# Sample convolution as POOL products with DVE sums, and prompt softmax normalised at its output, in a hybrid decoder step

## The chip, the core and the metric

The kernel runs on one core of a Trainium2 chip. The core has a matrix engine (TensorE, PE in the rows), two elementwise engines (VectorE, DVE; GpSimd, POOL), a table engine (ScalarE, ACT), a queue processor that starts transfers (SyncE, SP), and 16 DMA engines. Every engine runs its own instructions in the order in which they were written and waits on semaphores where it needs another's result. Only POOL can start the gathering transfers with a table of row indices; each costs POOL time of its own. The metric is the device time of one execution in microseconds. The granted clock of TensorE is told as a share of full speed: it changes between 1.2 and 2.4 GHz.

## What is computed

One layer of a decoder, for one prompt of 1024 tokens and for 8 sequences with 8 new tokens each (the sample): half a feed-forward, then attention beside a convolution, an output projection, and another half feed-forward.

```python
u = rms_norm(x) @ w_in              # query latent 384 | kv latent 256 | rope key 32 | conv 2 x 512
# group A: latent attention, 8 heads. Prompt: causal over 1024 tokens.
# Sample: over 4096 cached tokens in 32 pages of each sequence, and the 8 new ones
s = (q_abs @ c_kv.T + q_pe @ k_pe.T) * SM_SCALE
o = softmax(mask(s)) @ c_kv ; attn_out = o @ w_uv
# group B: convolution of width 31 along the tokens, 512 channels
g = ga * sigmoid(gb)
ext = concat([conv_state, g])       # 30 earlier rows (zeros for the prompt)
y = depthwise_conv(ext, w_dw) + b_dw    # y[t, ch] = b[ch] + sum over k of w_dw[k, ch] * ext[t + k, ch]
conv_out = silu(layer_norm(y))
x = x + concat([rms_norm(attn_out), rms_norm(conv_out)]) @ w_out
```

All data is fp32. The outputs are the new hidden states and the new cache entries.

## The kernel before

In time the kernel is: first feed-forward (to some 760 us in the trace), in-projection (to 905), the **sample stage** (905 to 1278), the **prompt attention** (1278 to 1487), out-projection (to 1640) and the second feed-forward. Large matrix products are done with fewer multiplications by adding operands first, so that three matmuls (lines 127, 128 and 129, `mm3`) stand for a product; DVE, ACT and POOL make the operand sums.

The order on every engine is settled when the program is built. A planner (`fl`) keeps a clock of estimated nanoseconds: generators yield the cost of the piece just written, `fl.add` starts a piece that runs beside the others, `fl.spend` lets the planned time pass, `fl.wait` lets it pass until pieces are done. A changed cost so moves the pieces of other work in the queues, and nothing is reordered on the chip.

**Sample stage.** `mgen` (line 1520) walks 32 steps, each with 1024 cached tokens of one sequence, two tiles of keys a half. `qk` multiplies queries with the keys `kst`, three quarters of which SP loads and one quarter POOL gathers (lines 1036, 1032), and DVE moves the scores to an SBUF tile `Ssb` from the pool `sb` (tag "S", LAG+2 = 7 buffers). `expo` and `trans` follow 4 and 5 steps later, and `pv` (line 1478) multiplies with the latents `cst` 6 steps later. All 128 `cst` tiles are gathered by POOL (line 1416, 7 buffers): when PE has read two tiles, the next two loads may start. Into this stream the planner fills other PE work: `w2` (line 1242, the conv inputs, matmuls `u<-h,w`, for four groups of 128 channels) and then `pprep` (keys and values of the prompt).

`conv_chunk` (line 1147) puts the convolution of one channel group into the queue `conv`: for each of 31 taps one DVE operation over the prompt's 1024 positions (input `gx`) and one over the sample's 64 (input `ge`, 8 sequences of 38 rows). The first tap is a `tensor_scalar` with the bias, the others are `scalar_tensor_tensor`, output `zc`. `conv_run` (line 1160) emits them one by one at their planned costs of 1150 and 200 ns, and goes on with the layer norm of the convolution (`lnorm`, line 1176) in three column groups of 364, 364 and 360 tokens; its end is a tanh on ACT and two POOL `tensor_tensor` (tiles `th` and `zc`, lines 1225 to 1230) for each of the four channel groups.

**Prompt attention.** 16 units, each a block of 256 queries (i = 0 to 3) and a pair of heads p. `stage_a` makes the queries `qf` (PE, then DVE with a table out of PSUM), `stage_b` the scores of the four (head e, half v) parts into SBUF tiles `P`, with L = 128 to 1024 keys. `soft` (line 1616) is the minimum, ACT's exp with the row sum (line 1620), DVE's reciprocal (line 1622), and a scaling of all of P by it: on DVE for v = 0 (line 1627), on ACT for v = 1 (line 1625, `P<-P,s` of line 116). `stage_c` (line 1630) transposes P in 128 x 128 pieces on PE (`T_`, line 1643) into a PSUM bank of kind "t" (three banks), moves them to SBUF (`pt`, DVE at line 1650 or ACT), and multiplies with the values (`PV`, line 1658) into the single bank of kind "o"; ACT moves that to `at` (line 1670). The units overlap: while unit u makes its scores, unit u+1 makes its queries and unit u-1 is in `stage_c`. The functions follow as they were.

Of the kernel before, what the change touches and what calls it, by code (L numbers as in the profile page):

```python
# [103 lines left out]
def body(ctx, tc, A):  # L104
# [1014 lines left out]
    def qhead():  # L1119
# [14 lines left out]
        for c in range(3):  # L1134
            m = 96 if c < 2 else 64
            for e in range(2):
# [5 lines left out]
                yield 850.0  # L1142


    conv = deque()

    def conv_chunk(i, gx, ge):
        for k in range(CW):
            wk = wdw[:, i, k:k + 1]
            for o, g, ns in ((zc[:, i, 0:S], gx[:, k:k + S], 1150.0),  # L1150
                             (zc[:, i, S:N].rearrange("p (b t) -> p b t", t=T), ge[:, :, k:k + T], 200.0)):
                if k == 0:
                    conv.append((ns, lambda o=o, g=g, wk=wk: dve.tensor_scalar(
                        out=o, in0=g, scalar1=wk, scalar2=b_dw[:, i:i + 1], op0=ALU.mult, op1=ALU.add)))
                else:
                    conv.append((ns, lambda o=o, g=g, wk=wk: stt(o, g, wk, o, ALU.mult, ALU.add)))

    share = [0.0]

    def conv_run():  # L1160
        done = 0
        while done < 4 * 2 * CW:
            if conv:
                ns, op = conv.popleft()
                op()
                done += 1
                yield ns / share[0]
            else:
                yield 300.0
        yield from lnorms()  # L1170
# [71 lines left out]
    def w2():  # L1242
        for i in range(4):
            while len(conv) > 2 * (CW if i > 1 else 2 * CW):
                yield None
# [30 lines left out]
    es_kv, es_q = ExitStack(), ExitStack()  # L1276
    kT, at_ = [], {}

# [126 lines left out]
    cp, sb, ptp, sm = op("cp", CBUF), op("sb", LAG + 2), op("ptp", 2), op("sm", 2)  # L1405
    B = {}

    def load_c():
# [133 lines left out]
    for d in mgen():  # L1542
        fl.spend(d)
        due += d * (KV_RATE if at_ else FILL_RATE)
        while fill is not None and due > 0.0:
# [38 lines left out]
    def stage_a(u):  # L1584
        i, p = units[u]
        U[u] = dict(q=[], P={}, pt={}, soft=[])
        for e in range(2):
# [10 lines left out]
    def stage_b(u):  # L1598
        i, p = units[u]
        for e in range(2):  # L1600
            for v in range(2):
                qt = 2 * i + v
                L = (qt + 1) * 128
                P = pp.tile([128, S], F32, tag="P", name="P")
                mn, s_, rs = (sm.tile([128, 2], F32, tag=f"s{j}", name=f"s{j}") for j in range(3))
                for j, k0 in enumerate(range(0, L, 512)):
# [5 lines left out]
                U[u]["P"][e, v] = P  # L1612
                U[u]["soft"].append(fl.add(soft(P, L, v, mn, s_, rs), L * 1.69 + 900.0))
                yield L * 1.69

    def soft(P, L, v, mn, s_, rs):
        if L > 512:
            tt(mn[:, 0:1], mn[:, 0:1], mn[:, 1:2], ALU.min)
            yield 300.0
        act.activation(out=P[:, :L], in_=P[:, :L], func=AF.Exp, scale=-1.0, bias=mn[:, 0:1], accum_out=s_[:, 0:1])  # L1620
        yield 900.0 +  0.4 * L
        dve.reciprocal(out=rs[:, 0:1], in_=s_[:, 0:1])
        if v:
            yield 300.0
            acopy(P[:, :L], P[:, :L], rs[:, 0:1])
        else:
            dve.tensor_scalar(out=P[:, :L], in0=P[:, :L], scalar1=rs[:, 0:1], scalar2=None, op0=ALU.mult)
        yield 0.0

    def stage_c(u):  # L1630
        i, p = units[u]
        fl.wait(*U[u]["soft"])
        o = bank("o")[:, :256]
        P, pt = U[u]["P"], U[u]["pt"]

        def T_(e, jj):
# [26 lines left out]
        for jj in range(i + 3):  # L1663
            if jj <= i:
                T_(1, jj)
                yield 430.0
            if jj > 1:
                PV(jj - 2)
                yield 860.0
        acopy(at[:, p, i * 256:i * 256 + 256], o)  # L1670
        U.pop(u)
# [10 lines left out]
    for u in range(len(units) + 1):  # L1682
# [8 lines left out]
        if u:  # L1691
            other.append(stage_c(u - 1))
            cost += (units[u - 1][0] + 1) * 1720.0
        done = 0.0
# [101 lines left out]
KBUF, CBUF = 6, 7  # L1796
LAG = 5
BIG = 3e38

# [95 lines left out]
```

## Time and profile before

| | us |
|---|---|
| three runs, median (lowest, highest) | 2372.63 (2364.92, 2373.29) |
| the profiled execution, its own time | 2358.99 |
| its span from first to last instruction | 2357.2 |
| PE busy in the span | 2178.0 (92%) |
| DVE, ACT, POOL busy | 1568.2, 843.8, 1063.3 |
| mean granted clock of TensorE | 0.967 |

The profiled execution is 13.6 us below the median of the runs, and 1.8 us of it lie outside its span. A busy engine says little by itself: what a stage is worth is read from the waits of PE in that stage and from what ended them, and PE's clock falls where it had to wait. All rows named below are from this one execution.

### The profile page before, as it was taken

Reading aid. Unit: us, or ns where it says so; the run is one execution under the profiler, and the core shown is the slowest. Engines: PE = TensorE matmul, PEld = TensorE weight load, DVE = VectorE, ACT = ScalarE, POOL = GpSimd, SP = SyncE. Lnnn points to the kernel's source line nnn. Section 1 sums busy time; section 2 is a strip of 40 time slices with the busy share of each in tenths; the row PEclk is TensorE's granted clock in tenths of the full one; section 3 lists DMA queues with packets and bytes.
Section 4 is the critical chain, followed back from the end, with each engine's and each line's share of the span. In section 5 each row is a group of like instructions: output and inputs, shape, how many; then the busy total and the mean of one; then the engine's idle time right before and its main releaser. Section 6 shows DMA issues by size and latency. Waiting matters only on the chain. (4 is left out here: it accounts for less than half of the span.)

```text
span 2357.2 us, 42356 instructions
## 1 busy us (share of the span) xinstructions
PE 2178.0 (92%) x15714; PEld 1999.7 (85%) x15714; DVE 1568.2 (67%) x3061; ACT 843.8 (36%) x1759; POOL 1063.3 (45%) x995
## 2 busy tenths in 40 slices
PE   6989999999999898997688999899799999999997
PEld 6989999999999796785455765799799999999996
DVE  7976666666565666996533776577866656766567
ACT  4332222234344421211233656543332222334343
POOL 3446676631134303675455322343456777411234
PEclk8999999999999998998888999999999999999998
DMA  4126676648654434888575000452166666458653
GB/s 147 51 82 212 203 228 200 210 144 291 225 193 161 128 124 133 227 244 234 169 225 157 14 1 18 139 194 92 61 195 209 212 219 211 131 194 285 210 170 122
DMA packets 252527, 392.69 MB, mean 167 GB/s; under 512 B 26912, under 2 KB 188064, under 8 KB 252192
## 3 DMA queue, kind: packets, MB, share of 16 engines
q1 hardware_dynamic: 153184, 261.23, 35.2%
q10 hardware_dynamic: 85824, 85.75, 10.6%
q0 software_dynamic: 13312, 43.00, 6.3%
q8 instruction: 124, 2.03, 0.4%
q14 instruction: 83, 0.68, 0.1%
HBM read 299.71 MB, written 90.19 MB: 165 GB/s over the span
## 5 line engine op out<-in xcount | busy, mean ns | idle before, releaser
L110 DVE TENSOR_TENSOR wh<-wst,wh 128x512 fp32r<-128x512 f32 x355 | 302.7, 861 | 281.6 <-ACT wh L116 280.7
L110 POOL TENSOR_TENSOR ts<-ts 128x272 f32<-128x272 f32 (+1 forms) x352 | 309.3, 879 | 314.4 <-DMA ts<-a_dram 197.7
L127 PE MATMUL gu<-h,wh 128*128 128x272 f32 x1248 | 361.9, 290 | 11.9 <-DVE m L110 9.8
L128 PE MATMUL gu<-h,wh 128*128 128x272 f32 x1248 | 361.0, 289 | 4.0 <-DVE h L110 4.0
L129 PE MATMUL gu<-h,wh 128*128 128x272 f32 x1248 | 360.9, 289 | 1.2 <-DVE wh L110 1.2
L116 ACT ACTIVATE wh<-wst 128x512 fp32r<-128x512 f32 x355 | 217.9, 624 | 398.7 <-PE d L129 167.2
L127 PE MATMUL d<-h,wh 128*128 128x272 f32 x1232 | 355.5, 289 | 0.0
L128 PE MATMUL d<-h,wh 128*128 128x272 f32 x1232 | 353.9, 287 | 0.0
L129 PE MATMUL d<-h,wh 128*128 128x272 f32 x1232 | 353.8, 287 | 0.0
L127 PE MATMUL gu<-t,wh 128*128 128x272 f32 x936 | 273.5, 292 | 18.3 <-DVE sg L110 11.5
L129 PE MATMUL gu<-t,wh 128*128 128x272 f32 x936 | 271.7, 290 | 3.0 <-DVE wh L110 3.0
L128 PE MATMUL gu<-t,wh 128*128 128x272 f32 x936 | 271.2, 290 | 2.7 <-DVE t L110 2.7
L127 PEld LDWEIGHTS gu<-h,wh 128*128 128x128 f32 x1248 | 235.8, 189 | 14.7 <-DVE m L110 12.4
L128 PEld LDWEIGHTS gu<-h,wh 128*128 128x128 f32 x1248 | 235.9, 189 | 4.7 <-DVE h L110 4.7
L129 PEld LDWEIGHTS gu<-h,wh 128*128 128x128 f32 x1248 | 235.7, 189 | 1.4 <-DVE wh L110 1.4
L127 PEld LDWEIGHTS d<-h,wh 128*128 128x128 f32 x1232 | 231.6, 188 | 0.4
L128 PEld LDWEIGHTS d<-h,wh 128*128 128x128 f32 x1232 | 231.6, 188 | 0.2
L129 PEld LDWEIGHTS d<-h,wh 128*128 128x128 f32 x1232 | 231.4, 188 | 0.0
L1416 POOL DMA_INDIRECT cst<-in_cN,c_rep x128 | 142.5, 1113 | 182.2 <-DVE qx L1141 83.5
L127 PEld LDWEIGHTS gu<-t,wh 128*128 128x128 f32 x936 | 177.7, 190 | 22.4 <-DVE sg L110 14.4
L127 PE MATMUL u<-h,w 128*128 128x364 f32 (+3 forms) x528 | 183.0, 347 | 2.0 <-ACT h L116 2.0
L129 PEld LDWEIGHTS gu<-t,wh 128*128 128x128 f32 x936 | 177.7, 190 | 3.2 <-DVE wh L110 3.2
(260 smaller groups left out, 4884.9 us busy)
## 6 DMA issues: line engine op xcount, KB each, us to landing
wst<-in_wgu SPq DMA_DIRECT2D x88, 512.0 KB
kst<-in_kT SPq DMA_DIRECT2D x192, 144.0 KB
t_dram<-ts ACTq DMA_DIRECT2D x44, 544.0 KB
ts<-in_wd SPq DMA_DIRECT2D x88, 256.0 KB
a_dram<-acc ACTq DMA_DIRECT2D x78, 272.0 KB
wst<-s_dram SPq DMA_DIRECT2D x40, 512.0 KB
ast<-t_dram SPq DMA_DIRECT2D x66, 272.0 KB
s_dram<-ts ACTq DMA_DIRECT2D x44, 384.0 KB
```

The lines of the kernel that those rows point to most:

```text
L110: eng.tensor_tensor(out=out, in0=a, in1=b, op=op)
L116: act.activation(out=out, in_=a, func=AF.Copy, scale=scale)
L127: pe.matmul(out, ah, bh, start=first, stop=False)
L128: pe.matmul(out, ah, bl, start=False, stop=False)
L129: pe.matmul(out, al, bh, start=False, stop=last)
L1416: pool.indirect_dma_start(out=t.rearrange("p a c -> p (a c)"), out_offset=None, in_=A["cN"], in_offset=bass.IndirectOffsetOnAxis(ap=cidx[: ...
```

## The change

Two things are changed. **In the sample's convolution** the 31 DVE operations of a channel group on 64 positions become four POOL multiplications, four DVE reductions and one DVE addition of the bias. Each multiplication takes two sequences: an overlapping view of `ge` (for each of 8 positions the 31 inputs that its taps read) times the 31 taps, broadcast, gives 2 x 8 x 31 = 496 products a partition; the tile `cwin` for them comes from the score pool `sb`, tag "S". They are put into the queue `conv` behind the prompt's taps 8, 13, 18 and 23, and each is summed one such place later. The queue of a channel group has 40 entries in place of 62. The prompt's taps stay as they are. `at_` is moved up, and the test for the values becomes `"V" in at_`, with the same meaning.

**In the prompt attention** P stays unscaled. The four row sums of a unit stand in one tile; DVE takes the reciprocal of the four at once and spreads each over 64 columns (`rw`), PE transposes the two 128 x 128 halves into a bank of kind "t", ACT moves that to SBUF (`rb`), and the move of the output to `at` becomes a DVE multiplication `at = o * rb`. The planned costs follow: `soft` ends with the exp, and `stage_c` has 220 ns more.

```diff
 def conv_chunk(i, gx, ge):
     for k in range(CW):
         wk = wdw[:, i, k:k + 1]
-        for o, g, ns in ((zc[:, i, 0:S], gx[:, k:k + S], 1150.0),
-                         (zc[:, i, S:N].rearrange("p (b t) -> p b t", t=T), ge[:, :, k:k + T], 200.0)):
...
+        o, g = zc[:, i, 0:S], gx[:, k:k + S]
...
+        if k in SPOTS:
+            sconv(i, SPOTS.index(k), ge)
+def sconv(i, j, ge):
+    if 0 < j <= DB // 2:
+        o = zc[:, i, S + 2 * (j - 1) * T:S + 2 * j * T].rearrange("p (b t) -> p b t", t=T)
+        conv.append((600.0, lambda: dve.tensor_reduce(out=o, in_=prod.pop((i, j - 1)), axis=AX.X, op=ALU.add)))
+    if j < DB // 2:
+        def make():
+            g = ge[:, 2 * j:2 * j + 2, 0:T]
+            win = bass.AP(g.tensor, g.offset, [*g.ap, [1, CW]])
+            w = wdw[:, i].unsqueeze(1).unsqueeze(1).to_broadcast([128, 2, T, CW])
+            t = at_["sb"].tile([128, 512], F32, tag="S", name="cwin")[:, :2 * T * CW]
+            t = prod[i, j] = t.rearrange("p (b t k) -> p b t k", b=2, k=CW)
+            tt(t, win, w, ALU.mult, pool)
+        conv.append((0.0, make))
+    if j == DB // 2 + 1:
+        o2 = zc[:, i, S:N]
+        conv.append((200.0, lambda: dve.tensor_scalar(out=o2, in0=o2, scalar1=b_dw[:, i:i + 1], scalar2=None, op0=ALU.add)))
...
-    while done < 4 * 2 * CW:
+    while done < 4 * (CW + DB + 1):
...
+SPOTS = (8, 13, 18, 23, 28, 30)
...
 def soft(P, L, mn, s_):
...
-    dve.reciprocal(out=rs[:, 0:1], in_=s_[:, 0:1])
-    if v:
-        yield 300.0
-        acopy(P[:, :L], P[:, :L], rs[:, 0:1])
-    else:
-        dve.tensor_scalar(out=P[:, :L], in0=P[:, :L], scalar1=rs[:, 0:1], scalar2=None, op0=ALU.mult)
...
 def stage_c(u):
+    dve.reciprocal(out=rs.rearrange("p v e -> p (v e)"), in_=U[u]["sums"].rearrange("p v e -> p (v e)"))
+    wide = sm.tile([128, 2, 2, 64], F32, tag="rw", name="rw", bufs=2)
+    dve.tensor_copy(wide, rs.unsqueeze(3).to_broadcast([128, 2, 2, 64]))
+    rb = sm.tile([128, 256], F32, tag="rb", name="rb", bufs=2)
+    def spread_sums():
+        ps = bank("t")[:, :256]
+        for v in range(2):
+            pe.transpose(ps[:, v * 128:v * 128 + 128], wide[:, v].rearrange("p e d -> p (e d)"), ident)
+        acopy(rb, ps)
...
+            if jj == 1:
+                spread_sums()
+                yield 220.0
...
-        acopy(at[:, p, i * 256:i * 256 + 256], o)
+        tt(at[:, p, i * 256:i * 256 + 256], o, rb, ALU.mult)
```

The instructions stand as follows on the engines. First POOL early in the sample stage, before (the rows give line, operation, tiles and size; `mn` and `sums` are the sample attention's statistics):

```order
L1425 MEMSET mn 128x5
L1426 MEMSET sums 128x5
L1032 DMA kst<-in_kT,c_prep 96x384 x8
L1425 MEMSET mn 128x5
L1426 MEMSET sums 128x5
L1032 DMA kst<-in_kT,c_prep 96x384 x6
L1416 DMA cst<-in_cN,c_rep 128x512 x4
```

The same place with the change:

```order
L1449 MEMSET mn 128x5
L1450 MEMSET sums 128x5
L1032 DMA kst<-in_kT,c_prep 96x384 x2
L110 TENSOR_TENSOR cwin<-ge,c_wdw 128x496
L1032 DMA kst<-in_kT,c_prep 96x384 x2
L110 TENSOR_TENSOR cwin<-ge,c_wdw 128x496
L1032 DMA kst<-in_kT,c_prep 96x384 x4
L110 TENSOR_TENSOR cwin<-ge,c_wdw 128x496
L1449 MEMSET mn 128x5
L1450 MEMSET sums 128x5
```

The products stand between the gathers, four to each channel group, 16 in all.

POOL at the end of the sample stage, before (`th` and `zc` are the end of the layer norm of the first 364 tokens):

```order
L1032 DMA kst<-in_kT,c_prep 96x384 x2
L1416 DMA cst<-in_cN,c_rep 128x512 x25
L110 TENSOR_TENSOR th<-th,zc 128x364
L110 TENSOR_TENSOR zc<-zc,th 128x364
L110 TENSOR_TENSOR th<-th,zc 128x364
L110 TENSOR_TENSOR zc<-zc,th 128x364
```

The same place with the change:

```order
L1032 DMA kst<-in_kT,c_prep 96x384 x2
L1440 DMA cst<-in_cN,c_rep 128x512 x20
L110 TENSOR_TENSOR th<-th,zc 128x364
L110 TENSOR_TENSOR zc<-zc,th 128x364
L110 TENSOR_TENSOR th<-th,zc 128x364
L110 TENSOR_TENSOR zc<-zc,th 128x364
L1440 DMA cst<-in_cN,c_rep 128x512 x4
L110 TENSOR_TENSOR th<-th,zc 128x364
L110 TENSOR_TENSOR zc<-zc,th 128x364
L1440 DMA cst<-in_cN,c_rep 128x512
L110 TENSOR_TENSOR th<-th,zc 128x364
L110 TENSOR_TENSOR zc<-zc,th 128x364
```

The convolution is planned to end earlier, so its layer norm comes earlier in the queue: four of the multiplications now stand ahead of the last five gathers, and two more ahead of the last one.

DVE around the last unit of the prompt attention, before (`s` are the sums, `pt` the transposed P):

```order
L1622 RECIPROCAL s_17303<-s_17302 128x1
L1627 TENSOR_SCALAR P<-P,s_17303 128x896
L110 TENSOR_TENSOR s_17326<-s_17326 128x1
L1622 RECIPROCAL s_17328<-s_17327 128x1
L1650 COPY pt_17356<-t 128x512
L1650 COPY pt_17370<-t 128x512
```

The same place with the change:

```order
L110 TENSOR_TENSOR s_17155<-s_17155 128x1
L110 TENSOR_TENSOR at<-o,rb 128x256
L1654 RECIPROCAL rs<-s_16902 128x4
L1656 COPY rw<-rs 128x256
L1679 COPY pt_17184<-t 128x512
L1679 COPY pt_17198<-t 128x512
L110 TENSOR_TENSOR at<-o,rb 128x256
```

The scaling of P is gone, one reciprocal of the four sums and its spreading stand ahead of the copies out of the "t" banks, and the move of the output is now in DVE's queue.

## Rows read from the trace of the kernel before

**Rows 1.** Busy time of the engines by stretch of time, from the view of windows: stretch, length, PE, PEld, DVE, ACT, POOL, then the granted clock, the share of the DMA engines and GB/s.

```profile
905.00:960.00 55.00, 45.73 (x292) 34.91 (x291) 42.83 (x76) 7.06 (x13) 25.30 (x25) 0.88 0.62 172
960.00:1098.00 138.00, 135.86 (x991) 105.21 (x990) 124.91 (x237) 27.80 (x68) 99.27 (x95) 0.99 0.88 245
1098.00:1200.00 102.00, 60.28 (x354) 39.24 (x352) 46.86 (x87) 22.92 (x55) 41.61 (x39) 0.77 0.59 176
1200.00:1278.00 78.00, 68.11 (x445) 41.22 (x441) 25.19 (x76) 30.51 (x75) 50.25 (x54) 0.93 0.78 233
1278.00:1487.00 209.00, 195.39 (x1196) 133.86 (x1196) 146.62 (x512) 131.13 (x312) 57.61 (x59) 0.97 0.04 14
```

**Rows 2.** Waits of PE in the sample stage, from the view of waits of three stretches, in order: 960 to 1098, 1098 to 1200, 1200 to 1278. Columns: us in total, times, longest.

```profile
PE s L1434 <- DMA kst<-in_kT,c_prep: 1.3, 1, 1.3
...
PE s L1434 <- DMA kst<-in_kT: 36.1, 4, 12.6
PE s L1434 <- DMA kst<-in_kT,c_prep: 5.6, 1, 5.6
...
PE o L1491 <- DMA cst<-in_cN,c_rep: 6.2, 9, 1.9
```

**Rows 3.** The convolution on DVE, 905 to 1278, groups by operation and shape: count, busy us in all, mean ns of one, idle time before.

```profile
L113 DVE SCALAR_TENSOR_TENSOR zc<-gx,c_wdw,zc 128x1024 f32<-128x1024 f32 x120 | 153.0, 1275 | 0.0
L113 DVE SCALAR_TENSOR_TENSOR zc<-ge,c_wdw,zc 128x64 f32<-128x64 f32 x120 | 33.1, 276 | 0.0
```

**Rows 4.** Waits of POOL, 960 to 1098 (first row) and 1098 to 1200 (the other two).

```profile
POOL cst L1416 <- PE o L1491: 17.6, 13, 4.7
...
POOL cst L1416 <- PE o L1491: 39.1, 8, 14.8
POOL kst L1032 <- PE s L1434: 13.6, 2, 13.3
```

**Rows 5.** Groups of POOL instructions by shape: the gathers from 960 to 1098, then two shapes of `tensor_tensor` over the whole kernel. Columns as in rows 3.

```profile
L1416 POOL DMA_INDIRECT cst<-in_cN,c_rep x57 | 66.3, 1164 | 30.8 <-PE o L1491 17.6 <-issue 9.4 <-PE s L1434 2.0
L1032 POOL DMA_INDIRECT kst<-in_kT,c_prep x28 | 32.6, 1164 | 7.9 <-issue 7.0 <-PE t L1484 0.3 <-PE o L1491 0.3
...
L110 POOL TENSOR_TENSOR ts<-ts 128x256 f32<-128x256 f32 x176 | 151.0, 858 | 106.5 <-DMA ts<-in_wd 96.1
...
L110 POOL TENSOR_TENSOR s<-wst 128x512 f32<-128x512 f32 x78 | 111.4, 1429 | 53.5 <-DMA wst<-in_wgu 22.8 <-DVE wh L110 18.0 <-DVE acc L110 12.3
```

**Rows 6.** DVE's wait for POOL's fill of the statistics, 960 to 1098, from the view of waits.

```profile
DVE Ssb L1440 <- POOL sums L1426: 5.8, 2, 3.5
```

**Rows 7.** POOL's timeline at the end of the sample stage: start, duration, operation, and in brackets the idle time before it and what ended it.

```profile
1255.40 0.95 POOL L1416 DMA_INDIRECT cst<-in_cN,c_rep  x1 [3.57 <-PE o L1491]
...
1266.00 0.95 POOL L1416 DMA_INDIRECT cst<-in_cN,c_rep  x1 [0.30 <-DMA cst<-in_cN,c_rep]
...
1271.03 0.95 POOL L1416 DMA_INDIRECT cst<-in_cN,c_rep  x1 [0.30 <-PE t L1484]
1272.00 0.97 POOL L110 TENSOR_TENSOR th<-th,zc 128x364 f32<-128x364 f32 x1
1273.05 0.95 POOL L110 TENSOR_TENSOR zc<-zc,th 128x364 f32<-128x364 f32 x1
```

**Rows 8.** PE's timeline at the same place, to the first matmuls of the prompt attention.

```profile
1274.74 1.08 PE L1491 MATMUL o<-cst,spt 128*64 128x256 f32 x6 [0.80 <-DMA cst<-in_cN,c_rep]
1275.75 0.64 PE L1496 MATMUL o<-cx,ptn 64*64 64x256 f32 x2
1278.43 0.47 PE L1514 MATMUL t<-c_ident,om 64*128 64x64 f32 x2 [2.04 <-DVE om L1510]
1278.84 0.58 PE L127 MATMUL t<-qb,wq 128*128 128x256 f32 x1
```

**Rows 9.** Waits of PE in the prompt attention, 1278 to 1487.

```profile
PE t L1643 <- DVE pt L1650: 3.7, 4, 2.2
PE t L1643 <- DVE s L110: 2.3, 1, 2.3
...
PE t L1643 <- DVE v L113: 1.8, 1, 1.8
...
PE t L1643 <- DVE qf L110: 1.1, 3, 0.5
```

**Rows 10.** DVE and ACT groups in the prompt attention, forms taken together but for the third row, the query's multiplication out of PSUM.

```profile
L1627 DVE TENSOR_SCALAR P<-P,s 128x128 f32<-128x128 f32 (+3 forms) x32 | 19.6, 613 | 1.1
L1622 DVE RECIPROCAL s<-s 128x1 f32<-128x1 f32 x64 | 9.9, 157 | 5.3 <-ACT P L1620 5.3
...
L110 DVE TENSOR_TENSOR qf<-t,c_tabs 128x256 f32<-128x256 f32 x32 | 13.4, 419 | 9.0 <-PE t L129 8.8
...
L116 ACT ACTIVATE P<-P,s 128x256 f32<-128x256 f32 (+3 forms) x32 | 26.4, 826 | 24.5 <-DVE s L1622 24.4
```

**Rows 11.** PE's timeline: eleven transposes of P in a row.

```profile
1382.47 1.36 PE L1643 MATMUL t<-c_ident,P 128*128 128x128 f32 x11
```

**Rows 12.** Two timelines of one moment in the prompt attention: DVE, then POOL.

```profile
1374.52 0.55 DVE L1627 TENSOR_SCALAR P<-P,s 128x640 f32<-128x640 f32 x1
...
1407.09 1.25 DVE L1627 TENSOR_SCALAR P<-P,s 128x640 f32<-128x640 f32 x1
...
1406.13 4.03 POOL L110 TENSOR_TENSOR zc<-zc,bc 128x360 f32<-128x360 f32 x4 [20.95 <-ACT bc L116]
```

More of the change, by code (lines that the diff above doesn't have):

```diff
@@ L1142, in qhead @@
                 yield 850.0
+    at_ = {}
     conv = deque()
@@ L1149, in conv_chunk @@
             wk = wdw[:, i, k:k + 1]
-            for o, g, ns in ((zc[:, i, 0:S], gx[:, k:k + S], 1150.0),
-                             (zc[:, i, S:N].rearrange("p (b t) -> p b t", t=T), ge[:, :, k:k + T], 200.0)):
-                if k == 0:
-                    conv.append((ns, lambda o=o, g=g, wk=wk: dve.tensor_scalar(
-                        out=o, in0=g, scalar1=wk, scalar2=b_dw[:, i:i + 1], op0=ALU.mult, op1=ALU.add)))
-                else:
-                    conv.append((ns, lambda o=o, g=g, wk=wk: stt(o, g, wk, o, ALU.mult, ALU.add)))
+            o, g = zc[:, i, 0:S], gx[:, k:k + S]
+            if k == 0:
+                conv.append((1150.0, lambda o=o, g=g, wk=wk: dve.tensor_scalar(
+                    out=o, in0=g, scalar1=wk, scalar2=b_dw[:, i:i + 1], op0=ALU.mult, op1=ALU.add)))
+            else:
+                conv.append((1150.0, lambda o=o, g=g, wk=wk: stt(o, g, wk, o, ALU.mult, ALU.add)))
+            if k in SPOTS:
+                sconv(i, SPOTS.index(k), ge)
+    prod = {}
+    def sconv(i, j, ge):
[14 more added lines that the diff above has]
+            conv.append((200.0, lambda: dve.tensor_scalar(out=o2, in0=o2, scalar1=b_dw[:, i:i + 1], scalar2=None, op0=ALU.add)))
     share = [0.0]
@@ L1243, in w2 @@
         for i in range(4):
-            while len(conv) > 2 * (CW if i > 1 else 2 * CW):
+            while len(conv) > (CW + DB + 1) * (1 if i > 1 else 2):
                 yield None
@@ L1276, in body @@
     es_kv, es_q = ExitStack(), ExitStack()
-    kT, at_ = [], {}
+    kT = []
     def hold(ns):
@@ L1406, in body @@
     B = {}
+    at_["sb"] = sb
     def load_c():
@@ L1543, in body @@
         fl.spend(d)
-        due += d * (KV_RATE if at_ else FILL_RATE)
+        due += d * (KV_RATE if "V" in at_ else FILL_RATE)
         while fill is not None and due > 0.0:
@@ L1585, in stage_a @@
         i, p = units[u]
-        U[u] = dict(q=[], P={}, pt={}, soft=[])
+        U[u] = dict(q=[], P={}, pt={}, soft=[], sums=sm.tile([128, 2, 2], F32, tag="s1", name="s1"))
         for e in range(2):
@@ L1604, in stage_b @@
                 P = pp.tile([128, S], F32, tag="P", name="P")
-                mn, s_, rs = (sm.tile([128, 2], F32, tag=f"s{j}", name=f"s{j}") for j in range(3))
+                mn = sm.tile([128, 2], F32, tag="s0", name="s0")
                 for j, k0 in enumerate(range(0, L, 512)):
@@ L1612, in stage_b, with soft @@
                 U[u]["P"][e, v] = P
-                U[u]["soft"].append(fl.add(soft(P, L, v, mn, s_, rs), L * 1.69 + 900.0))
+                U[u]["soft"].append(fl.add(soft(P, L, mn, U[u]["sums"][:, v, e:e + 1]), L * 1.69 + 900.0))
                 yield L * 1.69
-    def soft(P, L, v, mn, s_, rs):
+    def soft(P, L, mn, s_):
         if L > 512:
@@ L1619, in soft @@
             yield 300.0
-        act.activation(out=P[:, :L], in_=P[:, :L], func=AF.Exp, scale=-1.0, bias=mn[:, 0:1], accum_out=s_[:, 0:1])
-        yield 900.0 +  0.4 * L
-        dve.reciprocal(out=rs[:, 0:1], in_=s_[:, 0:1])
-        if v:
-            yield 300.0
-            acopy(P[:, :L], P[:, :L], rs[:, 0:1])
-        else:
-            dve.tensor_scalar(out=P[:, :L], in0=P[:, :L], scalar1=rs[:, 0:1], scalar2=None, op0=ALU.mult)
+        act.activation(out=P[:, :L], in_=P[:, :L], func=AF.Exp, scale=-1.0, bias=mn[:, 0:1], accum_out=s_)
         yield 0.0
@@ L1634, in stage_c @@
         P, pt = U[u]["P"], U[u]["pt"]
+        rs = sm.tile([128, 2, 2], F32, tag="rs", name="rs")
+        dve.reciprocal(out=rs.rearrange("p v e -> p (v e)"), in_=U[u]["sums"].rearrange("p v e -> p (v e)"))
[7 more added lines that the diff above has]
+            acopy(rb, ps)
         def T_(e, jj):
@@ L1692, in body @@
             other.append(stage_c(u - 1))
-            cost += (units[u - 1][0] + 1) * 1720.0
+            cost += (units[u - 1][0] + 1) * 1720.0 + 220.0
         done = 0.0
```

## The prediction

> **What bounds the kernel now.** I read the busy time by stretch first, to see which engine fills which stretch, then the waits of PE in each stretch, then the timelines where a wait stands. In the sample stage there are three different limits. From 960 to 1098 PE is busy 135.86 of 138.00 us at a clock of 0.99 [rows 1] and waits in all 1.3 us for a POOL gather of keys [rows 2]: PE is the bound, although DVE with 124.91 and POOL with 99.27 plus its issue gaps are close behind. From 1098 to 1200 PE is busy 60.28 of 102.00 us, and 36.1 + 5.6 us of its waits end with transfers of keys [rows 2]; DVE is busy 46.86 us. From 1200 to 1278 the waits are for the latents that POOL gathers, 6.2 us in 9 waits [rows 2], and they come at the end: POOL issues its last loads one each 1.26 us (1266.00 to 1271.03 in four steps) and PE's last products of the sample wait for them, until 1274.74 [rows 7, 8]. In none of the three does a wait of more than 1 us of PE on DVE stand in the views, the one on `om` behind the last product apart [rows 8]. In the prompt attention PE is busy 195.39 of 209.00 us [rows 1]; what it lacks is mostly waits for DVE, 3.7 + 2.3 + 1.8 + 1.1 = 8.9 us at the transposes and the query's products [rows 9].
>
> **Convolution: what DVE loses.** 120 taps of 276 ns are 33.1 us [rows 3], and four first taps of about the same size make some 34 us. Added are 16 reductions over 496 inputs and 4 additions; no reduction of this size is in the rows read, so I bound one by the 128x64 tap (0.28 us) and the query's product of 256 columns doubled (0.84 us): 5 to 14 us. DVE is relieved by 20 to 29 us. I cost that at nothing: in the sample stage PE doesn't wait for DVE, and the work that hides it is PE's own 135.86 us and then the transfers. If that cover were gone, the 20 to 29 us would be the gain's ceiling.
>
> **Convolution: what POOL gets.** 16 products of 128x496. POOL's `tensor_tensor` takes 858 ns for 256 columns and 1429 for 512 [rows 5]; by the larger, 496/512 x 1429 = 1.39 us each, 22 us in all. The view with overlapping rows and four levels has no row. Below, 0.86 us is the end; above, I take twice the 1429, 2.9 us, since a collision with DVE doubles an operation in this trace: a scaling of 128x640 took 1.25 us while POOL multiplied, and 0.55 without [rows 12]. I take 1.39, the nearest shape. By the order 4 products lie ahead of 960, 8 from 960 to 1098, 4 from 1098 to 1200. In the middle stretch POOL's queue holds 57 + 28 gathers; its only slack is the 17.6 us in which it waits until PE has read a tile [rows 4]. 8 x 1.39 = 11.1 us go into that slack, but a product delays what is queued behind it: the gathers of `cst` and `kst`, and the fills of `mn` and `sums` for which DVE waited 5.8 us already [rows 6]. PE is six steps behind the loads, so most is absorbed. From 1098 to 1200 POOL idles 39.1 + 13.6 us behind PE [rows 4], so 4 x 1.39 = 5.6 us fit, unless they stand ahead of the gather for which PE waited 5.6 us. I take **+2**, with 0 and +8 as ends (8: 8 x 2.9 = 23.2 less 17.6 is 5.6, and two products of 1.39 ahead of that gather).
>
> The Trainium skill, GPSIMD Engine Reference, section 1 (Specifications), states that POOL shares its SBUF interfaces with VectorE and contends with DVE instructions that have two SBUF inputs or run in a 2-port mode. The prompt's taps read `gx` and `zc`, so this speaks against the change, and the doubled scaling in rows 12 agrees with it; by it the products would be at their upper end, which is the second rival.
>
> **End of the sample stage.** The layer norm now comes earlier in POOL's queue: by the order two pairs of `th` and `zc` stand ahead of the last five gathers, a third pair ahead of the last. A pair took 0.97 + 0.95 us and the step from one to the next is 1.05 [rows 7], some 2 us a pair. The tanh that they wait for is ACT work which needs only the normalised convolution, and I expect it to be done. So the last gather starts 3 x 2 = 6 us later than 1271.03, and as PE already waits for these gathers and nothing else is left for it there, the first matmul of the prompt attention moves by the same: **+6**. The ends are +2 (PE's last products spread out so that only the third pair stands ahead of the last wait) and +9 (POOL waits for a tanh, half as much again).
>
> **Prompt attention.** Removed: 19.6 us of scaling and 9.9 us of reciprocals on DVE, 26.4 us of scaling on ACT [rows 10]. Added for each of 16 units: a reciprocal (0.16), a spread of 256 columns (at most the 0.42 of the query's product), and a multiplication of 128x256 out of PSUM (0.42) on DVE, together 16.0 us at most, so DVE is relieved by 29.5 - 16.0 = 13.5 us of 146.62; ACT loses 26.4 us and the move of the output, and gains a move of the same size, so nothing else. PE gets 32 transposes at 1.36/11 = 0.124 us [rows 11]: **+4.0**, on the path because PE is the bound here. Of the 8.9 us of waits for DVE, the copy `pt` (3.7) and the small minimum (2.3) stand behind scalings in DVE's queue, but also behind other work that stays (the norm's small steps, the query's product). What is late next where a scaling goes is that remaining queue, by 0.6 us less per scaling. I take a bit over half, **-5**; the ends are -8.9 with another -5 for a clock that stays at 1.00 rather than 0.97 (195.39 x 0.03 = 5.9), and +4: the reciprocal of four sums stands at the head of `stage_c` and holds the copies queued behind it on DVE until ACT's last exp, and the single "o" bank comes free through DVE's queue rather than ACT's, a quarter of a us a unit (16 x 0.25 = 4, and the +4.0 on top). Sum of the stage: -1, from -10 to +8. Everything after 1487 is the same code; I cost it at nothing.
>
> **Sum.** +2 +6 -1 = **+7 us**. On the profiled execution that is 2358.99 + 7 = 2366; it lies 13.6 us under the median of the runs, and against the median it is 2372.63 + 7 = 2379.6, say **2380 us**. Its own range: 0 to +17 from the terms not all at one end, 2372 to 2390.
>
> **Rivals.**
> 1. *The prompt attention gives more, and the end of the sample stage costs nothing.* PE's waits for DVE vanish and the clock stays up: -8.9 - 5.9 + 4.0 = -11, and if the planner's other moves let PE's last sample products run behind the gathers, the +6 falls to +1 and the products hide: -10 to -14, 2359 to 2363, take 2360. For it speaks that the waits for DVE have scalings right ahead of them; against it that the gathers are visibly the last wait at 1274.74.
> 2. *POOL becomes the bound* (slower). A product takes 2 us or more, by its form or by contention with DVE's taps. It decides from 17.6/8 = 2.2 us on: beyond that POOL can't follow PE from 960 to 1098. At 2.9 us: +5.6 there, 4 x 2.9 = 11.6 from 1098 to 1200 of which I let half stand ahead of gathers that PE waits for, +6, and the end's +6 to +8: +18 to +20 less 1, so 2390 to 2392. For it speaks rows 12; against it that gathers make up most of POOL's time and that 512 columns have a mean of 1429 ns next to a busy DVE.
> 3. *The end costs, but is paid back* (no change): the earlier norms leave the prompt attention's start to POOL, and the stage's gain is -6: about 2373.
> 4. *DVE holds the prompt attention*: each unit waits 0.5 to 1 us for the reciprocal or the "o" bank: +8 to +16, and +8 of the sample stage: 2389 to 2396.
>
> **How the numbers follow.** Forecast 0.40, rival 1 0.25, rival 2 0.17, rival 3 0.11, rival 4 0.07. The bound for a change that can be told from none is 0.5%, 11.9 us: 2360.8 to 2384.5. The forecast lies in it but for its upper fifth (0.08), rival 3 lies in it, rival 1 is cut in two by it (0.18 below, 0.07 inside), rivals 2 and 4 lie above but for 0.02. That gives faster 0.18, same 0.52, slower 0.30. The range leaves out about a tenth at either end: it goes from 2356, past rival 1's 2359 by the spread of its two largest terms, to 2396, rival 4's end.
>
> **What would show it.** In the profile after: the mean of the products on POOL (1.39 us, or over 2.2 for rival 2); POOL's waits until PE has read a tile from 960 to 1098 (17.6 falling to some 6); the last gather some 6 us later relative to the stage's start, with PE waiting for it; no wait of PE on DVE in the sample stage; the prompt attention at 208 us with fewer waits of the transposes on `pt`. Wrong would be the forecast if a stretch in which PE waits for transfers gets longer or shorter by over 5 us with the small moves in SP's order, for which no row gives a price, or if DVE's relief shortens the sample stage at all.

## The result and the profile after

The changed kernel is **slower by 0.78%**: median 2388.21 us (2379.53 to 2390.91, 7 runs) against 2368.97 us (2364.92 to 2377.87, 7 runs) of the kernel before on the same chip, ratio 1.0078 with a 95% interval of 1.0060 to 1.0096, some 19 us. The forecast was 2380 in a range of 2356 to 2396; the sign, slower by more than the 0.5% that can be told, had a chance of 0.30 in it.

The profiled execution after took 2390.91 us (span 2389.1), near its median; the one before lay 10 us under its own, so the two profiles differ by 32 us where the medians differ by 19. From the start of the first key product, of the first query product and of the first matmul of the out-projection on PE's timeline, the stages are:

| us | sample stage | prompt attention | out-projection to end |
|---|---|---|---|
| before, first profile | 372.5 | 208.8 | 869.6 |
| before, a second profile (run e0 below) | 372.9 | 206.2 | 866.3 |
| after | 408.0 | 201.8 | 872.0 |

The loss is in the sample stage, and the prompt attention gains; how much of the 35.5 us between these two profiles belongs to the change is taken up below. The windows of the profile after, columns as in [rows 1], in stretches cut at sequence boundaries of the sample, and the prompt attention last:

```profile
976.00:1068.00 92.00, 84.26 (x572) 63.80 (x568) 77.58 (x98) 16.72 (x41) 66.49 (x60) 0.93 0.77 212
1068.00:1105.00 37.00, 34.98 (x259) 26.56 (x261) 32.15 (x55) 6.51 (x19) 30.04 (x27) 1.00 0.72 212
...
1232.00:1315.00 83.00, 63.88 (x362) 37.07 (x358) 19.86 (x61) 25.30 (x61) 49.31 (x53) 0.83 0.64 190
1315.00:1517.00 202.00, 194.05 (x1228) 136.97 (x1228) 136.02 (x464) 109.50 (x281) 51.42 (x53) 0.98 0.05 15
```

and the same sequences (the third to the fifth) in the profile before, in one row:

```profile
975.00:1087.00 112.00, 112.00 (x828) 87.86 (x825) 103.93 (x199) 23.45 (x58) 83.46 (x78) 1.00 0.88 244
```

Before, PE did these 828 matmuls in 112 us without a pause at a clock of 1.00. After, 831 took 92 + 37 = 129 us. The waits of PE after in these 92 us, then in the stage's last 83 us, name what is new (columns as in [rows 2]):

```profile
PE s L1458 <- DVE mn L1464: 5.2, 1, 5.2
PE t L1497 <- ACT olT L116: 2.5, 1, 2.5
...
PE o L1515 <- DMA cst<-in_cN,c_rep: 9.5, 6, 4.0
PE t L1497 <- ACT Ssb L1484: 3.2, 1, 3.2
```

There are two places. The first is one that the prediction said didn't exist: PE waits **for DVE** in the sample stage, before the first key product of the fourth sequence. DVE's timeline of the changed kernel there, ahead of the score operation that PE waits for, then POOL and PE:

```profile
1011.09 3.92 DVE L113 SCALAR_TENSOR_TENSOR zc<-gx,c_wdw,zc 128x1024 f32<-128x1024 f32 x3
1014.93 0.66 DVE L1167 TENSOR_REDUCE zc<-cwin 128x16 f32<-128x496 f32 x1
1015.51 1.27 DVE L113 SCALAR_TENSOR_TENSOR zc<-gx,c_wdw,zc 128x1024 f32<-128x1024 f32 x1
1016.71 0.53 DVE L110 TENSOR_TENSOR gx<-u,sg 128x364 f32<-128x364 f32 x1
1017.15 2.72 DVE L113 SCALAR_TENSOR_TENSOR zc<-gx,c_wdw,zc 128x1024 f32<-128x1024 f32 x1
1019.80 0.68 DVE L1464 CUSTOM_DVE_ANT_0 Ssb<-s,zero 128x512 f32<-128x512 f32 x1
...
1017.59 1.20 POOL L110 TENSOR_TENSOR cwin<-ge,c_wdw 128x496 f32<-128x496 f32 x1
...
1020.54 2.90 PE L1458 MATMUL s<-kst,qx 96*64 96x256 f32 x12 [5.20 <-DVE mn L1464]
```

The scores were finished at 1013.3, and DVE came to them at 1019.8, 6.5 us late. A tap that takes 1.275 us in [rows 3] took 2.72 us, and a POOL product of 1.20 us lies inside it. But DVE was late before: four steps earlier (step 7 of the 32, the last of the second sequence) it stood idle for 8.86 us and began on the scores 4.7 us after PE's last key product had ended. `remote` means that no instruction in the profile ended this wait. The profile before has no such delay at this step. The rows are after, then before, PE's key products and DVE's operation on them:

```profile
967.75 1.51 PE L1458 MATMUL s<-kst,qx 96*64 96x256 f32 x12
973.96 0.69 DVE L1464 CUSTOM_DVE_ANT_0 Ssb<-s,zero 128x512 f32<-128x512 f32 x1 [8.86 <-remote]
...
967.15 1.51 PE L1434 MATMUL s<-kst,qx 96*64 96x256 f32 x12
968.84 0.69 DVE L1440 CUSTOM_DVE_ANT_0 Ssb<-s,zero 128x512 f32<-128x512 f32 x1 [1.39 <-PE s L1434]
```

This delay is not made by the change: run e2, whose instructions in the sample stage are those of the kernel before, has it too. The profiles after, e1 to e5, e8 and e11 have it (3.2 to 4.9 us); before, e0, e6, e7, e9 and e10 are at most 0.2 us late there. The profiles also differ in PE's idle time in the sample stage for which they name no cause (`issue`): none before, in e0, e9 and e10, and 3.4 to 14.6 us in the others, 9.1 after and 12.6 in e2. What makes either stays open.

Behind the wait the clock is lower: 0.71 in the 11.5 us after it, where the profile before had 1.00 at the same work. The rows are after, then before:

```profile
1020.50:1032.00 11.50, 11.46 (x62) 9.39 (x64) 8.70 (x15) 2.07 (x4) 5.88 (x8) 0.71 0.49 144
...
1014.00:1024.00 10.00, 10.00 (x80) 7.96 (x76) 10.00 (x19) 2.25 (x4) 8.00 (x9) 1.00 0.76 233
```

Twelve key products took 2.90 us right after the wait, and 1.52 us later in the same step (1029.76): at the lower of the two clock levels what follows a stall takes nearly twice as long. The wait of 2.5 us for ACT (`olT`) stands behind a wait of the same unnamed kind, 7.81 us of ACT's.

The second place is the stage's end, as forecast. POOL's timeline after, answering to [rows 7], and PE's, answering to [rows 8]:

```profile
1295.27 0.95 POOL L1440 DMA_INDIRECT cst<-in_cN,c_rep  x1 [0.30 <-PE o L1515]
1296.23 0.97 POOL L110 TENSOR_TENSOR th<-th,zc 128x364 f32<-128x364 f32 x1
...
1299.23 0.95 POOL L110 TENSOR_TENSOR zc<-zc,th 128x364 f32<-128x364 f32 x1
1300.33 0.99 POOL L1440 DMA_INDIRECT cst<-in_cN,c_rep  x1
...
1305.10 0.96 POOL L110 TENSOR_TENSOR th<-th,zc 128x364 f32<-128x364 f32 x1
...
1307.23 0.98 POOL L1440 DMA_INDIRECT cst<-in_cN,c_rep  x1
...
1303.68 1.95 PE L1515 MATMUL o<-cst,spt 128*64 128x256 f32 x6 [3.99 <-DMA cst<-in_cN,c_rep]
...
1310.63 1.97 PE L1515 MATMUL o<-cst,spt 128*64 128x256 f32 x6 [2.18 <-DMA cst<-in_cN,c_rep]
```

Four multiplications keep the fifth load from the end back from 1296.2, where the load ahead of it ends, to 1300.33, two more hold the last one, and PE waits 3.99 and 2.18 us behind them. The added work, by groups of the profile after (products, sums, taps, then the additions to the prompt attention):

```profile
L110 POOL TENSOR_TENSOR cwin<-ge,c_wdw 128x496 f32<-128x496 f32 x16 | 21.5, 1343 | 0.3
...
L1167 DVE TENSOR_REDUCE zc<-cwin 128x16 f32<-128x496 f32 x16 | 10.6, 661 | 0.0
...
L113 DVE SCALAR_TENSOR_TENSOR zc<-gx,c_wdw,zc 128x1024 f32<-128x1024 f32 x120 | 158.5, 1320 | 2.3
...
L1656 DVE COPY rw<-rs 128x256 f32<-128x256 f32 x16 | 7.4, 463 | 0.5
L110 DVE TENSOR_TENSOR at<-o,rb 128x256 f32<-128x256 f32 x16 | 6.7, 419 | 8.3 <-PE o L1687 8.2
L1654 DVE RECIPROCAL rs<-s 128x4 f32<-128x4 f32 x16 | 2.7, 169 | 0.1
```

A product takes 1.34 us (forecast 1.39), a sum 0.66 us, and the prompt's 120 taps take 158.5 us rather than the 153.0 of [rows 3].

### The profile page after: what moved, and what is told of

Same layout as the page of the kernel before. It is cut to its first block, busy times and chain, and to the rows that moved or that the text cites. A ratio compares the mean times of both kernels' runs of the same rounds, so it can differ in the third digit from the quotient of the medians.

```text
span 2389.1 us, 42328 instructions
## 1 busy us (share of the span) xinstructions
PE 2199.3 (92%) x15746; PEld 2017.9 (84%) x15746; DVE 1549.2 (65%) x2909; ACT 821.7 (34%) x1727; POOL 1083.1 (45%) x1011
## 5 line engine op out<-in xcount | busy, mean ns | idle before, releaser
L1440 POOL DMA_INDIRECT cst<-in_cN,c_rep x128 | 152.5, 1191 | 196.8 <-DVE qx L1141 83.6
```

Source lines behind the costliest of these rows:

```text
L1440: pool.indirect_dma_start(out=t.rearrange("p a c -> p (a c)"), out_offset=None, in_=A["cN"], in_offset=bass.IndirectOffsetOnAxis(ap=cidx[: ...
```

## The experiments

Runs e1, e2, e4 and e5 shared one chip, e3, e6, e7 and e8 another, e9, e10 and e0 a third, e11 a fourth. The kernel before had medians of 2371.8, 2368.4, 2355.0 and 2373.1 us there, so the comparisons go by the ratio to it, and a difference between two ratios from different chips is less certain than one from the same chip. What the expectations call theory one is that the loss lies in the changed order of the work; theory two, that it lies in the products on POOL. A diff is against the changed kernel where nothing else is said.

**e1, the convolution part alone.** The functions of the prompt attention are those of the kernel before.

```diff
-def soft(P, L, mn, s_):
+def soft(P, L, v, mn, s_, rs):
...
+    dve.reciprocal(out=rs[:, 0:1], in_=s_[:, 0:1])
...
-    tt(at[:, p, i * 256:i * 256 + 256], o, rb, ALU.mult)
+    acopy(at[:, p, i * 256:i * 256 + 256], o)
```

> The convolution part alone; the prompt softmax as in the kernel before. By the two traces the sample stage is longer with the change and the prompt attention 7 us shorter. If the two parts add up, this kernel is about 26 us slower than the kernel before (some 2395 us against 2369), with a prompt attention of 208 to 209 us. Rival: the prompt attention's 7 us come from the earlier norms of the convolution and not from the softmax; then the time is as that of the changed kernel, about 2388, with a prompt attention of 202 us.

Measured: 2387.33 us, ratio 1.0064 (1.0045 to 1.0083); sample stage 400.5 us, prompt attention 205.3. The convolution part makes the loss. The 26 us that I had read off the two profiles were too many, since the profile before lay under its median.

**e2, the softmax part alone.** `conv_chunk`, `conv_run` and `w2` are those of the kernel before.

```diff
-    while done < 4 * (CW + DB + 1):
+    while done < 4 * 2 * CW:
```

> The softmax part alone; the convolution as in the kernel before. If the two parts add up: about 7 us faster than the kernel before, some 2362 us, prompt attention about 202 us, sample stage unchanged at about 372 us. Rival as above: no difference, about 2369, prompt attention 208 us.

Measured: 2368.57 us, ratio 0.9977 (0.9960 to 0.9995); prompt attention 202.2 us. The softmax part is a gain of 0.23%, some 5 us, and its stage is as short as in the changed kernel. The sample stage of this profile was 387.2 us, though its instructions stand there as in the kernel before: one execution can be 15 us longer there than another. That makes e2 the better partner for the profile after, which has the same delay of DVE and unnamed idle time of PE: against it the sample stage is 20.8 us longer after, 13.7 us of it between the new tokens' scores of the third and of the fourth sequence (52.6 against 38.9 us for the same matmuls) and 4.8 us at the stage's end.

**e4, the whole change planned at the old cost.** Only the planned cost of a tap is different.

```diff
...
-            conv.append((1150.0, lambda o=o, g=g, wk=wk: stt(o, g, wk, o, ALU.mult, ALU.add)))
+            conv.append((1266.0, lambda o=o, g=g, wk=wk: stt(o, g, wk, o, ALU.mult, ALU.add)))
```

> The whole change, but the planned cost of each tap of the prompt is 1266 ns in place of 1150, so that a channel group is planned at the 41850 ns that it had before. The layer norm then stands behind all gathers again, and the matmuls of the conv inputs and of the keys come about where they stood before; the products stay on POOL. Theory one (the moved order costs, the products themselves little): sample stage 372 to 378 us, 2363 to 2370 in all. Theory two (the products in POOL's queue cost): only the 6 us of the norm's end come back, about 2382.

Measured: 2363.55 us, ratio **0.9969** (0.9949 to 0.9990); sample stage 376.1 us. PE, ACT and SP have the order of the kernel before through the sample stage, DVE and POOL carry the changed convolution, and the loss of 0.78% is a gain of 0.31%. PE's waits in the third to fifth sequence are short:

```profile
PE s L1458 <- DMA kst<-in_kT,c_prep: 2.1, 1, 2.1
PE s L1458 <- DVE mn L1464: 2.0, 2, 1.6
```

**e5, the products on DVE.** The order of PE and SP is that of the changed kernel.

```diff
-            tt(t, win, w, ALU.mult, pool)
+            tt(t, win, w, ALU.mult, dve)
```

> The changed kernel with its 16 products on DVE in place of POOL, the order of PE and SP word for word the same. Theory one (moved order): no difference to the changed kernel, about 2388. Theory two (products in POOL's queue): sample stage shorter by what they cost there, about 2376, with the 6 us at the stage's end still there; DVE gets 16 x about 0.6 us.

Measured: 2385.66 us, ratio 1.0063 (1.0043 to 1.0084), not to be told from the changed kernel. PE still waits 4.5 us for DVE in the third to fifth sequence. Taken with e4 this looked like a clear answer for the order. It isn't: a product on DVE takes 0.66 us of DVE, and on POOL it costs DVE something too, 158.5 us for the prompt's taps against 153.0.

```profile
L110 DVE TENSOR_TENSOR cwin<-ge,c_wdw x16: 655/666/670, 915.2 to 1176.0; 128x496 f32<-128x496 f32 x16
...
PE s L1458 <- DVE mn L1464: 4.5, 2, 4.0
```

**e8, the moved order without the change.** The kernel before with a planned cost lowered.

```diff
-                             (zc[:, i, S:N].rearrange("p (b t) -> p b t", t=T), ge[:, :, k:k + T], 200.0)):
+                             (zc[:, i, S:N].rearrange("p (b t) -> p b t", t=T), ge[:, :, k:k + T], 84.0)):
```

> The kernel before, with all its 62 taps of a channel group on DVE and the softmax as it was; only the planned cost of a sample tap is 84 ns in place of 200, so that a channel group is planned at the 38250 ns of the changed kernel. Nothing is computed otherwise. Theory one (the moved order alone makes the loss): slower than the kernel before by as much as the convolution part alone, 2383 to 2390, with PE waits for DVE before score matmuls around the fourth sequence and two pairs of multiplications ahead of the last five gathers. Theory two (products, reductions and the tile in the score pool): about 2372, no difference but for the 6 us of the stage's end, 2378 at most.

Measured: 2376.5 us, ratio 1.0034 (1.0014 to 1.0054). That is half of e1's loss (the two intervals overlap a little) and falls between the two expectations. The stage's end shows the same waits as in the changed kernel (11.2 us for latents); in the third to fifth sequence PE waits for DVE only 1.9 us. So the order alone makes a loss, and probably not all of it: with the same order the new convolution of e1 costs 0.30% more than the old one here.

**e3, the stage's end repaired.** The order of the other matmuls stays moved.

```diff
+        while nload["c"] < DB * NG:
+            yield 200.0
         for k in range(4):
             th = scr.tile([128, n], F32, tag="nt", bufs=5, name="th")
```

> The changed kernel, but the tanh part of the first layer norm waits in the plan until all gathers of latents are issued, so that no multiplication stands ahead of a gather at the stage's end; the matmuls of the conv inputs and of the keys stay where the change put them. If the end costs the 6 us of the forecast: about 2382. If the end costs more (late clock, ACT's tanh ahead of the last exps): 2374 to 2378. If it costs nothing because something else is late next: 2388.

Measured: 2379.7 us, ratio 1.0048 (1.0031 to 1.0066), 0.30% or 7 us under the changed kernel (the two intervals overlap a little), and PE's waits for latents at the stage's end fall from 9.5 to 2.8 us:

```profile
PE o L1517 <- DMA cst<-in_cN,c_rep: 2.8, 2, 1.8
```

**e6, the convolution part alone, planned as before.** The edit is that of e1 and of e4 together.

> The convolution part alone, planned at the old 41850 ns a channel group; softmax as before. Theory one: the convolution part is worth nothing by itself, DVE's relief being off the path: 2368 to 2374. Were DVE's relief worth something in the sample stage, it would be under 2366.

Measured: 2368.41 us, ratio 1.0000 (0.9986 to 1.0015). With the old order the new convolution is worth nothing and costs nothing that can be measured: DVE's relief is off the path. The gain of e4 is then the softmax part's.

**e7, every product twice**, on the kernel of e4.

```diff
             tt(t, win, w, ALU.mult, pool)
+            tt(t, win, w, ALU.mult, pool)
```

> The whole change planned as before (as in the run planned at 1266 ns a tap), and every product made twice by POOL into the same tile. POOL gets 16 x 1.34 = 21 us more, some 11 of it between 960 and 1098. If the products hide in POOL's waits: 2363 to 2366, no more than 3 us over the run with single products. If POOL's queue is at its limit: 2370 to 2380.

Measured: 2383.09 us, ratio 1.0047 (1.0029 to 1.0064), against 0.9969 for e4, more than either expectation. From the third to the fifth sequence PE waits 7.6 + 4.6 = 12.2 us for gathers, where e4's waits for 2.1: POOL comes late with them. POOL's own wait until PE has read a tile does not show a limit, 7.6 us here and 4.7 in e4. The prompt's taps grew too, to 173.2 us from 164.1 in e4. Rows for PE:

```profile
PE o L1516 <- DMA cst<-in_cN,c_rep: 7.6, 3, 3.3
PE s L1459 <- DMA kst<-in_kT,c_prep: 4.6, 2, 3.0
PE s L1459 <- DVE mn L1465: 2.8, 1, 2.8
```

**e9, no products and no sums**, on the kernel of e3. The kernel leaves out 30 of the sample's 31 taps: one DVE operation a channel group makes the first tap and the bias. PE, SP and ACT have the order of e3.

```diff
-        conv.append((600.0, lambda: dve.tensor_reduce(out=o, in_=prod.pop((i, j - 1)), axis=AX.X, op=ALU.add)))
+        conv.append((600.0, lambda: None))
...
-        conv.append((0.0, make))
+        conv.append((0.0, lambda: None))
...
```

> As the run with the tanh behind the loads (the change with its moved order, the stage's end repaired; 2379.7 there), but without the 16 products and the 16 sums: the sample's convolution has only its first tap and the bias, so 30 of its 31 taps are left out. All else stands where it stood, with the same planned costs. If PE's wait of 5 us before the first key product of the fourth sequence comes from DVE's queue falling behind by the sums and by taps that a product on POOL stretches: DVE then reaches the score of step 11 within 4 us of its matmuls, the wait is gone, and the time is 2366 to 2372. If it comes from where the matmuls stand on PE alone: the wait stays over 3 us and the time over 2375.

Measured: 2357.01 us, ratio 1.0006 (0.9991 to 1.0021). Against e3 that is 0.42%, 10 us. PE's wait for DVE before the fourth sequence is gone. But so is the delay of DVE at step 7 (0.2 us, 4.7 in e3), which the edit does not touch and which no profile from the third chip has; the run does not part the two. DVE's timeline at the place shown of the changed kernel:

```profile
1007.13 3.92 DVE L113 SCALAR_TENSOR_TENSOR zc<-gx,c_wdw,zc 128x1024 f32<-128x1024 f32 x3
1010.97 0.53 DVE L110 TENSOR_TENSOR gx<-u,sg 128x364 f32<-128x364 f32 x1
1011.42 1.27 DVE L113 SCALAR_TENSOR_TENSOR zc<-gx,c_wdw,zc 128x1024 f32<-128x1024 f32 x1
1012.61 0.68 DVE L1458 CUSTOM_DVE_ANT_0 Ssb<-s,zero 128x512 f32<-128x512 f32 x1
```

**e11, the products again, without the sums**, on the kernel of e9, on another chip.

```diff
...
-        conv.append((0.0, lambda: None))
+        conv.append((0.0, make))
```

> As the run without products and sums, but POOL makes the 16 products again; they are read by nobody, the sums stay left out, and the sample's convolution keeps its first tap and the bias only. It parts the two causes of DVE's lag. If the stretched taps alone do it: the wait of PE before the first key product of the fourth sequence is back with 2 to 5 us, and the time is 0.2% to 0.4% above the kernel before. If it needs the sums' 0.66 us each as well: no wait over 1 us there, and the time is within 0.15% of the run without both (1.0006 of the kernel before).

Measured: 2382.03 us, ratio 1.0040 (1.0022 to 1.0057). The wait is back, and 0.34 of the 0.42% with it, although nobody reads the products. I had taken that as the products' doing. But the delay of DVE at step 7 is back as well, 4.7 us, and the products add 1.4 us to it up to step 11. Against e3, which has the delay too, leaving out the sums changes nothing that can be told (1.0040 against 1.0048). The same tap as above on DVE, POOL's product, and PE's wait:

```profile
1018.57 2.73 DVE L113 SCALAR_TENSOR_TENSOR zc<-gx,c_wdw,zc 128x1024 f32<-128x1024 f32 x1
1021.22 0.68 DVE L1464 CUSTOM_DVE_ANT_0 Ssb<-s,zero 128x512 f32<-128x512 f32 x1
...
1019.02 1.19 POOL L110 TENSOR_TENSOR cwin<-ge,c_wdw 128x496 f32<-128x496 f32 x1
...
PE s L1458 <- DVE zc L113: 4.8, 1, 4.8
```

The following table is worked out from the timelines of DVE and PE: how long after the end of a step's key products DVE starts on the scores, in us, for the last step of the second sequence and the four of the third; PE's wait for DVE before the fourth; and the time from the new tokens' scores of the third sequence to those of the fourth, in which PE has the same matmuls in all of them.

| kernel | step 7 | 8 | 9 | 10 | 11 | PE's wait | stretch |
|---|---|---|---|---|---|---|---|
| before | 0.2 | 1.9 | 0.1 | 1.7 | 0.6 | 0 | 38.7 |
| e2, softmax alone, old convolution and order | 4.8 | 2.9 | 0.8 | 1.8 | 0.0 | 0 | 38.9 |
| e6, new convolution in the old order | 0.2 | 0.1 | 0.1 | 3.8 | 3.5 | 2.2 | 44.0 |
| e4, the change in the old order | 4.9 | 2.5 | 1.3 | 3.2 | 2.9 | 1.6 | 40.5 |
| e8, old convolution in a moved order | 3.2 | 3.3 | 3.1 | 3.1 | 3.2 | 1.9 | 43.7 |
| after | 4.7 | 4.0 | 3.8 | 5.0 | 6.5 | 5.2 | 52.6 |
| e5, products on DVE | 4.8 | 3.5 | 2.8 | 4.7 | 5.3 | 4.0 | 52.1 |
| e11, products, no sums | 4.7 | 4.1 | 3.8 | 5.1 | 6.1 | 4.8 | 48.8 |
| e9, neither | 0.2 | 1.5 | 0.1 | 1.1 | 0.7 | 0 | 38.3 |

Late at step 7 are all but before, e6 and e9. In the old order DVE makes up all of it with the old convolution (e2) and 2.0 us with the new (e4). In the moved order it makes up none with the old (e8) and loses 0.5 to 1.8 us more with the new (after, e5, e11). How the moved order does without such a delay only e9 shows, and it has neither products nor sums.

There are two PSUM banks for scores, and at the end of a sequence the new tokens' scores take one. So the next sequence's first product needs the bank that DVE still has to read. In the table a lag up to about 1.3 us is free there, and each us beyond it is one of PE's, with a lower clock after the long waits.

**e10, planned a little longer.** 1340 ns for a tap, 660 for a sum.

```diff
...
-            conv.append((1150.0, lambda o=o, g=g, wk=wk: stt(o, g, wk, o, ALU.mult, ALU.add)))
+            conv.append((1340.0, lambda o=o, g=g, wk=wk: stt(o, g, wk, o, ALU.mult, ALU.add)))
...
```

> The whole change, with 1340 ns planned for a tap of the prompt and 660 for a sum: the spacing of the taps is then as in the kernel before, and DVE has fewer other operations between them, so it should reach the scores earlier than in the run planned at 1266 ns. If DVE's lag behind the scores is what is left in that run: 1 to 4 us under its 2363.6. If the later end of the convolution and of its layer norm costs more than that: 2364 to 2372.

Measured: 2352.17 us, ratio 0.9982 (0.9969 to 0.9996). DVE is at the scores of the third sequence within 0.1 us, and still the ratio isn't under e4's; the two intervals overlap. Both versions beat both kernels.

**e0, the kernel before once more.**

> The kernel before once more, for a second profile: the first lies 13 us under the median of the runs. Its sample stage was 372.5 us; the kernel with only the softmax part, whose sample stage is built alike, had 387. If the difference is one between executions of the same program: a sample stage of some 380 to 390 us here, and a time of 2365 to 2375.

Measured: 2353.19 us, sample stage 372.9 us. My explanation missed: two profiles of the kernel before agree within 0.5 us in that stage. Both are of the kind without the delay of DVE and without idle time of PE that the profile names no cause for; e2's has both (4.8 and 12.6 us). Why one kind or the other comes, and whether it goes with the chip, stays open.

## Why the prediction was right and where it was wrong

The range held the time, and "slower" was said with 0.30, but the most likely case was "no change", and one step was wrong. That the range reached so far was partly luck: its upper part came from rivals 2 and 4, neither of which happened, and of the loss only the stage's end came about as it was priced.

- **"In none of the three does a wait of more than 1 us of PE on DVE stand", so of DVE's relief "I cost that at nothing".** The first half was true of the profile before and was taken to hold after. It failed: after, DVE is 6.5 us behind the scores at the end of the third sequence, PE waits 5.2 us and then runs at the lower clock. DVE was busy 124.91 of 138.00 us there [rows 1], and I never asked how fast it can make up a delay. Of the 6.5 us, 4.7 were there at step 7, from a wait that no row explains and that e2 has too; the moved order no longer let DVE make them up (e8), and the new work added 1.8. One part of that is a product that held a tap up, 2.72 rather than 1.275 us. That the products alone make the wait, as e11 against e9 seemed to say, is not shown.
- **The products, +2 (0 to +8).** Their size was right, 1.34 against 1.39 us. In the old order they cost nothing that can be measured (e6: 1.0000), though the taps took 162.6 us there. In the moved order the new convolution costs 0.30% or 7 us more than the old (e1 against e8, the intervals overlap a little), and e5 shows the same loss with the products on DVE. So the term was near its upper end, by another road than the one priced. The sign given for it missed: POOL's wait until PE has read a tile was to fall from 17.6 us to some 6, and was 17.9 between 976 and 1105.
- **Rival 2, POOL as the bound from 2.2 us a product on.** It would have given 2390 to 2392, and the time was 2388, but its mechanism did not happen at 1.34 us: PE's waits for gathers between 976 and 1105 come to 0.8 us in the profile after. At 2 x 1.34 = 2.7 us PE does wait for gathers, 12.2 us in e7. The contention of the Trainium skill, GPSIMD Engine Reference, section 1 (Specifications), was weighed there as a price on POOL; the trace shows it on both sides: five taps, which have two SBUF inputs, took 1.6 to 2.7 us, and products beside the other taps took up to 1.55.
- **The stage's end, +6 (+2 to +9).** Right: e3 is 7 us under the changed kernel, and PE's waits for latents fall by 6.7 us. POOL had not to wait for a tanh, as assumed.
- **The prompt attention, -1 (-10 to +8).** The sign was right and the size too small. e2 gives -0.23%, some 5 us (-1 to -9). The waits of the transposes on DVE are 4.9 + 0.6 + 0.6 us after, against 8.9 in [rows 9]. Rival 4 did not happen: the single "o" bank shows no wait.
- **The moved order.** The prediction said that no row gives a price for the small moves in SP's order, and that it would be wrong if a stretch in which PE waits for transfers changed by over 5 us with them. The moved order did cost, but most where PE is the bound. e8 gives the order alone, the stage's end with it, as 0.34%; e4 shows that with the old order the whole change is a gain of 0.31%.

The sum on the chip: 7 us for the stage's end (e3), some 14 in the stretch before the fourth sequence's end (after against e2, by one profile each; 7.7 of it PE's waits for DVE and ACT, the rest the lower clock), -5 for the softmax: 16 of the 19. The other 3 us are within the spread of the profiles. That the moved order is needed for the loss is shown (e1 against e6, the changed kernel against e4); why DVE was late at step 7, and how large the loss is in an execution without that delay, stays open.

## What to carry to other kernels

An engine that nobody waits for can still have no slack: read how late it comes to the operation that frees a shared buffer and how fast it makes up a delay, not only whether someone waits for it. Work moved to another engine can still cost the first: with the products on POOL the taps on DVE took 158.5 to 164.1 us in place of 153.0. Where planned costs set the order, a lighter piece of work with a lower cost moves everything around it; keep the old cost in one run, so that the work and the order are measured apart. And before two profiles are set side by side, look whether both have the same delays that no instruction explains: here the run that seemed to settle the cause (e9) had lost one that its edit did not touch.

## What the hardware showed that I had not expected

- A DVE tap on 128x1024 with two SBUF inputs, 1.275 us alone, took up to 2.73 us around a POOL product of 1.2 us. In the profile after, two products that began 0.3 and 0.4 us into a tap held it up so (2.58 and 2.72 us); those that began some 0.8 us into it left it at 1.28 to 1.29 and took 1.5 us themselves. Over 120 taps the sum was 158.5 us against 153.0.
- A 5.2 us wait of PE cost more than 5.2 us: the granted clock was 0.71 over the next 11.5 us, and twelve key products took 2.90 us in place of 1.52.
- A POOL multiplication of 496 columns through an overlapping view with broadcast took 1.17 to 1.55 us; a plain one of 512 columns takes 1.43 on average [rows 5]; the same on DVE took 0.66 us, and so did the sum of 16 times 31.
